# A two-layer hybrid diffusion trunk: adaLN row sums on VectorE with a broadcast silu, and the inverse's small products issued round the array's tiles

## The chip, the cores and the metric

The kernel runs on one core of one Trainium2 chip. The metric is the device time of one execution in microseconds (us), as the median of the runs shown. TensorE is called PE, VectorE DVE, ScalarE ACT, GpSimd POOL; SP only issues the DMAs.

## The reference, cut to what matters

Two layers of a trunk over 512 latent tokens and 256 context tokens, with 1024 channels. Each layer modulates its normed input by vectors that come out of one matrix-vector product (adaLN), mixes by neighbourhood attention, a gated delta rule in chunks and a Fourier mixer, and ends in an MLP.

```python
cs, ccs = jax.nn.silu(c), jax.nn.silu(c_ctx)          # two vectors of 1024
...
sh1, sc1, gt1, sh2, sc2, gt2 = jnp.split((cs @ w_ada + b_ada)[:, None, :], 6, axis=-1)   # w_ada 1024 x 6144 a layer
n_mod = 6 if ctx_out else 2                           # the last layer needs two of the six for the context
cmod = jnp.split((ccs @ w_ada[:, :n_mod * d] + b_ada[:n_mod * d])[None, None, :], n_mod, axis=-1)
h_l = _rmsnorm(x, norm1) * (1 + sc1) + sh1
...
a_mat = strictly lower part of (kb @ k.T * decay) + eye(64)     # one for each chunk of 64 tokens, head and direction
sol = lax.linalg.triangular_solve(a_mat, rhs, left_side=True, lower=True)
...
x = x + gt1 * y_l
x = x + gt2 * _sq_relu_mlp(_rmsnorm(x, norm2) * (1 + sc2) + sh2, w_mlp1, w_mlp2)
```

All arithmetic is f32. The modulation needs 6144 sums of 1024 products a layer, once for the latent tokens and once for the context.

## The kernel before, in words

Activations lie channel-major: a tile has 128 channels on the partitions and 512 (latent) or 768 (latent and context) tokens along the row. Every weight tile is split into two rounded parts, `whi` (cast on ACT, line 233) and `wlo` (subtracted on DVE or POOL, line 236), and a projection is three matmuls for each of 8 contraction tiles (`proj`, line 245). There are 4 buffers of raw weights (`wr`) and 3 of split ones, each half a unit (4 contraction tiles).

The program runs start, layer 0, layer 1. A layer has three stretches: the Fourier mixer and the first head's input; the mix, in which four streams (delta rule, its preparation, attention, input projections) are interleaved by `by_clock`; and the main stretch, with the gated merge of three branches (loop over `bi`), the output projection (`ps_wo`), the second norm (`mod_norm`) and the MLP (`ps_m`). In the merge each of 8 tiles `k` takes a gate (`ps_in`, computed there for the first branch, read back as `sgg` for the others) and a branch product (`ps_br`); lines 1082 to 1085 multiply and add them on DVE, and line 253 splits the sum `y` into `ysh`, `ysl` for the output projection. A list scheduler in the framework sets the order on each engine by the program's order as priority and by its own estimate of readiness; each engine then works through its list in order.

**adaLN.** 4 blocks of 512 outputs are made at the start (`ada_block`). The other 20 blocks are made in layer 0's main stretch: a generator, `ada_rest`, is advanced by `ada_tick` (ADA_RATE 0.6 steps for each projection unit), and by `ada_upto` where a result is due. `ada_group` makes 4 blocks at a time: for each of 8 contraction tiles it loads four tiles of `w_ada` (128x512) and issues four matmuls onto the array's four column strips, which hold the two silu vectors as a 32-column weight (line 168); then ACT copies the sums (172), four small matmuls against `sel8` turn them into columns (176), and DVE adds the bias (178).

**The inverse.** For each head and layer, `dn_prep` inverts 12 unit lower triangular 128x128 tiles (two 64-token chunks each): DVE inverts the 32x32 diagonal blocks of all at once (lines 581, 583), DMAs put them back as diagonal blocks, and PE merges. First 32 to 64: 24 products for R (line 601, a loop over two places q of the array, ACT copy 603 after each), then 36 for W (609, 613, again one place after the other, copies 616 and 617). Then 64 to 128: 12 products (625), and 6 at one place (630) and 6 at another (636), each with its PSUM tile and copy. An f32 product is two records in the trace.

Of the kernel before, what the change touches and what calls it, by code (L numbers as in the profile page):

```python
# [9 lines left out]
F32 = mybir.dt.float32  # L10
# [7 lines left out]
P = 128  # L18
D = 1024
# [12 lines left out]
WRAW, WSPLIT, WADA = 4, 3, 8  # L32
# [4 lines left out]
ADA_RATE, ADA_LAG = 0.6, 1  # L37
# [7 lines left out]
def kernel(ctx: ExitStack, tc: tile.TileContext, A: dict, out: bass.AP):  # L45
# [18 lines left out]
    def U(name, dt=F32, tag="u", w=TT):  # L64
        b, n = cur[tag]
        return b.tile([P, w], dt, tag=tag, bufs=n, name=name)
# [21 lines left out]
    def ps_aux(name, tag="pa"):  # L88
        b, n = cur["ps"]
        return b.tile([P, 512], F32, tag=tag, bufs=n[tag], name=name)  # L90

    def cload(name, shape, src):
        t = const.tile(shape, F32, name=name)
        sp.dma_start(out=t, in_=src)
        return t
# [17 lines left out]
    sel8 = cload("sel8", [P, 8], A["sel8"])  # L113
# [42 lines left out]
    def ada_group(l, q, lag):  # L156

        ps = ps_aux("ps_ada")
        ws = []
        for t in range(KD + lag):  # L160
            if t < KD:
                ws.append([U("wada", tag="wada", w=512) for _ in range(4)])
                for j in range(4):
                    sp.dma_start(out=ws[t][j], in_=A["wa"][l, q + j, t])
            if t >= lag:
                k = t - lag
                for j in range(4):
                    pe.matmul(ps[32 * j:32 * j + 32, :], lhsT=cs[:, k, :], rhs=ws[k][j], start=(k == 0),
                              stop=(k == KD - 1), tile_position=(0, 32 * j))
            yield  # L170
        asb = tp.tile([P, 512], F32, tag="t2", name="asb")
        act.copy(asb, ps)
        yield
        pm = ps_aux("ps_ada2")
        for i in range(4):
            pe.matmul(pm[:, 8 * i:8 * i + 8], lhsT=asb[:, i * P:(i + 1) * P], rhs=sel8, start=True, stop=True)
        b = vecs[l][:, V_BADA + 4 * q:V_BADA + 4 * q + 16].rearrange("p (j i) -> p j i", i=4)
        dve.tensor_tensor(MOD[l][:, 4 * q:4 * q + 16, :].rearrange("p (j i) s -> p j i s", i=4),
                          pm[:, 0:32].rearrange("p (i j s) -> p j i s", i=4, s=2),
                          b.unsqueeze(3).to_broadcast([P, 4, 4, 2]), op=ALU.add)  # L180
# [3 lines left out]
    def ada_scale(l, i, k0=0, n=KD):  # L184

        sc = MOD[l][:, (3 * i + 1) * 8 + k0:(3 * i + 1) * 8 + k0 + n, :]
        g = vecs[l][:, (V_N1, V_N2)[i] + k0:(V_N1, V_N2)[i] + k0 + n]
        o = SC[l][i][:, k0:k0 + n, :]
        dve.tensor_scalar(o, sc, 1.0, None, op0=ALU.add)
        dve.tensor_tensor(o, o, g.unsqueeze(2).to_broadcast([P, n, 2]), op=ALU.mult)  # L190

    def ada_rest():
        for l, qs, sc in ((0, (4, 8), (1,)), (1, (0, 4, 8), (0, 1))):
            for q in qs:
                yield from ada_group(l, q, ADA_LAG)
                ada_done.append((l, q + 3))
            for i in sc:
                ada_scale(l, i)
        ada_done.append((2, 0))
        while True:  # L200
            yield
# [163 lines left out]
    def layer(l):  # L365
# [158 lines left out]
        def dn_prep(h, st):  # L524
# [71 lines left out]
            R = U("R", tag="pr", w=NU * 64).rearrange("p (u c) -> p u c", c=64)  # L596
            ps = ps_aux("ps_r", "pp")
            for q in range(2):
                a, b = slice(64 * q, 64 * q + 32), slice(64 * q + 32, 64 * q + 64)
                for u in range(NU):  # L600
                    pe.matmul(ps[a, u * 32:u * 32 + 32], lhsT=Nu[b, u, a], rhs=Tst[b, u, b], start=True, stop=True,
                              tile_position=(64 * q + 32, 64 * q))
                act.copy(R[a, :, 0:32], ps[a, 0:NU * 32].rearrange("p (u c) -> p u c", c=32))
            ps = ps_aux("ps_w", "pp")
            for q in range(2):
                a, b = slice(64 * q, 64 * q + 32), slice(64 * q + 32, 64 * q + 64)
                ul = slice(0, NU) if q == 0 else slice(6, NU)
                for u in range(ul.start, ul.stop):
                    pe.matmul(ps[b, u * 32:u * 32 + 32], lhsT=R[a, u, 0:32], rhs=Nu[a, u, a], start=True, stop=True,
                              tile_position=(64 * q, 64 * q + 32))  # L610
                ut = slice(0, 6) if q == 0 else slice(0, NU)
                for u in range(ut.start, ut.stop):
                    pe.matmul(ps[a, u * 32:u * 32 + 32], lhsT=Nu[a, u, a], rhs=R[a, u, 0:32], start=True, stop=True,
                              tile_position=(64 * q, 64 * q))
                pv = ps[:, 0:NU * 32].rearrange("p (u c) -> p u c", c=32)
                act.activation(out=Nu[b, ul, a], in_=pv[b, ul], func=AF.Copy, scale=-1.0)
                act.activation(out=Tst[a, ut, b], in_=pv[a, ut], func=AF.Copy, scale=-1.0)
# [11 lines left out]
            for u in range(6):  # L629
                pe.matmul(ps[a, u * 64:u * 64 + 64], lhsT=Nu[a, u, a], rhs=R[a, u, :], start=True, stop=True,  # L630
                          tile_position=(0, 0))
            act.activation(out=Tst[a, 0:6, b], in_=ps[a, 0:384].rearrange("p (u c) -> p u c", c=64), func=AF.Copy,
                           scale=-1.0)
            ps = ps_aux("ps_w3", "pp")
            for u in range(6):
                pe.matmul(ps[b, u * 64:u * 64 + 64], lhsT=R[a, 6 + u, :], rhs=Nu[a, 6 + u, a], start=True, stop=True,
                          tile_position=(0, 64))
# [418 lines left out]
        main_scope = scope("main", u=27, t3b=3, wada=WADA)  # L1056
# [53 lines left out]
        ada_upto(*((0, 11), (2, 0))[l])  # L1110
        mh, ml = mod_norm(l, 1, x2, W, "m")
        fin = None if full else Rms(TL, ps_rms())
# [62 lines left out]
    for half in range(2):  # L1175
        k0, k1 = 4 * half, 4 * half + 4
        for q in (half, half + 2):
            ada_block(0, q)
        ada_scale(0, 0, k0, 4)
        if half == 0:  # L1180
            load_wab(0)
            ahead[0, T_DNK] = wload(A["wi"][0, T_DNK])
        hs += [modulate(k, xs[k]) for k in range(k0, k1)]
        layer.h = tuple(zip(*hs))
        if half == 0:
            for (s0, s1), ps, pb in zip(ALL, begun["in"], begun["ab"]):
                proj(ps, ahead[0, T_DNK], KD, *layer.h, [(s0, s1)], s0, 0, k1)
                proj_ab(pb, *layer.h, s0, s1, 0, k1)
    ident = cload("ident", [P, P], A["ident"])
# [13 lines left out]
def _prepare(inp):  # L1203
# [16 lines left out]
    r["wa"] = a["w_ada"].reshape(2, KD, P, 12, 512).transpose(0, 3, 1, 2, 4)  # L1220
# [53 lines left out]
    r["sel8"] = (i[:, None] // 32 * 2 + i[:, None] % 32 == np.arange(8)[None]) & (i[:, None] % 32 < 2)  # L1274
# [21 lines left out]
```

## Time and profile before

| | us |
|---|---|
| median of 3 runs (lowest, highest) | 2735.25 (2735.04, 2742.7) |
| profiled execution, its own time | 2732.88 |
| span of its instructions | 2731.1 |
| PE / DVE / ACT / POOL busy in it | 2567.2 / 1405.7 / 1191.6 / 619.5 |
| layer 0 mix, 200 to 755: PE / DVE busy | 513.7 / 379.8 of 555 |
| layer 0 main, 755 to 1480: PE / DVE busy | 722.0 / 237.8 of 725 |
| layer 1 mix, 1700 to 2250: PE / DVE busy | 497.6 / 370.4 of 550 |

The profiled execution's own time is 1.8 us above its span, and 2.4 us under the median. [...] A timeline row gives start and duration in us, then the group; a span of pipelined matmuls contains overlaps, so that the start of the next group tells more than a duration. In the groups by shape, the last figure ahead of the bar's end is the mean in ns of one.

### The profile page before, as it was taken

Reading aid. Unit: us, or ns where it says so; the run is one execution under the profiler, and the core shown is the slowest. Engines: PE = TensorE matmul, PEld = TensorE weight load, DVE = VectorE, ACT = ScalarE, POOL = GpSimd, SP = SyncE. Lnnn points to the kernel's source line nnn. Section 1 sums busy time; section 2 is a strip of 40 time slices with the busy share of each in tenths; the row PEclk is TensorE's granted clock in tenths of the full one; section 3 lists DMA queues with packets and bytes.
Section 4 is the critical chain, followed back from the end, with each engine's and each line's share of the span. In section 5 each row is a group of like instructions: output and inputs, shape, how many; then the busy total and the mean of one; then the engine's idle time right before and its main releaser. Section 6 shows DMA issues by size and latency. Waiting matters only on the chain. (4 is left out here: it accounts for less than half of the span.)

```text
span 2731.1 us, 40072 instructions
## 1 busy us (share of the span) xinstructions
PE 2567.2 (94%) x15066; PEld 2083.0 (76%) x15066; DVE 1405.7 (51%) x2847; ACT 1191.6 (44%) x2430; POOL 619.5 (23%) x522
## 2 busy tenths in 40 slices
PE   6998989899999999999999988898999999999998
PEld 3787868687888777888888867776777777688886
DVE  4657586858423634222222355769688436433334
ACT  4546555555644224122222255555565653423323
POOL 3221313131111112111111123322333222222222
PEclk9999999999999999999999999999999999999999
DMA  6232222222256743342321213232232336233322
GB/s 216 78 96 65 70 66 81 72 64 60 74 197 197 254 137 110 105 135 89 120 63 62 82 59 110 78 83 59 79 86 67 94 115 196 87 97 97 97 93 89
DMA packets 196706, 278.42 MB, mean 102 GB/s; under 512 B 56768, under 2 KB 75936, under 8 KB 196512
## 3 DMA queue, kind: packets, MB, share of 16 engines
q1 hardware_dynamic: 196512, 275.87, 32.6%
q8 instruction: 118, 1.93, 0.3%
q14 instruction: 76, 0.62, 0.1%
HBM read 244.29 MB, written 27.31 MB: 99 GB/s over the span
## 5 line engine op out<-in xcount | busy, mean ns | idle before, releaser
L236 POOL TENSOR_TENSOR wlo<-wr,whi 128x512 fp32r<-128x512 f32 x360 | 496.3, 1380 | 1849.8 <-ACT whi L233 1725.3
L233 ACT CAST whi<-wr 128x512 fp32r<-128x512 f32 x560 | 346.3, 619 | 869.5 <-PE ps_m L245 519.8
L245 PE MATMUL ps_in<-hh,whi 128*128 128x512 f32 x960 | 376.8, 403 | 10.5 <-ACT hh L325 4.7
L245 PE MATMUL ps_in<-hh,wlo 128*128 128x512 f32 x960 | 372.6, 399 | 0.8 <-POOL wlo L236 0.8
L245 PE MATMUL ps_in<-hl,whi 128*128 128x512 f32 x960 | 371.1, 397 | 0.0
L236 DVE TENSOR_TENSOR wlo<-wr,whi 128x512 fp32r<-128x512 f32 x200 | 138.6, 693 | 244.6 <-ACT whi L233 243.9
L245 PE MATMUL ps_m<-ml,whi 128*128 128x512 f32 (+1 forms) x768 | 233.9, 358 | 4.7 <-POOL ml L313 3.3
L245 PE MATMUL ps_m<-mh,whi 128*128 128x512 f32 (+1 forms) x768 | 232.6, 357 | 2.9 <-ACT mh L309 2.9
L245 PE MATMUL ps_m<-ah,wlo 128*128 128x512 f32 (+1 forms) x776 | 234.4, 355 | 0.0
L245 PE MATMUL ps_m<-ah,whi 128*128 128x512 f32 (+1 forms) x776 | 234.1, 355 | 0.0
L245 PE MATMUL ps_m<-al,whi 128*128 128x512 f32 (+1 forms) x776 | 233.1, 353 | 0.0
L245 PE MATMUL ps_m<-mh,wlo 128*128 128x512 f32 (+1 forms) x768 | 231.8, 355 | 0.0
L245 PEld LDWEIGHTS ps_in<-hh,whi 128*128 128x128 f32 x960 | 179.3, 191 | 42.9 <-ACT hh L325 4.8
L245 PEld LDWEIGHTS ps_in<-hh,wlo 128*128 128x128 f32 x960 | 178.5, 191 | 33.0 <-issue 1.6
L245 PEld LDWEIGHTS ps_in<-hl,whi 128*128 128x128 f32 x960 | 179.0, 191 | 30.5 <-issue 2.2
L1135 DVE SCALAR_TENSOR_TENSOR x<-ps_m,mod,x 128x512 f32<-128x512 f32 (+1 forms) x97 | 60.8, 654 | 248.1 <-PE ps_m L245 248.1
L245 PEld LDWEIGHTS ps_m<-mh,whi 128*128 128x128 f32 x768 | 126.4, 188 | 35.4 <-ACT whi L233 8.4
L245 PE MATMUL ps_inc<-hl,whi 128*128 128x256 f32 x512 | 149.8, 293 | 0.0
L245 PEld LDWEIGHTS ps_m<-ah,whi 128*128 128x128 f32 x776 | 127.7, 188 | 28.9 <-ACT whi L233 6.7
L245 PEld LDWEIGHTS ps_m<-ml,whi 128*128 128x128 f32 x768 | 126.7, 188 | 29.8 <-POOL ml L313 6.1
L245 PE MATMUL ps_inc<-hh,whi 128*128 128x256 f32 x512 | 149.3, 292 | 0.0
L245 PE MATMUL ps_inc<-hh,wlo 128*128 128x256 f32 x512 | 148.1, 289 | 0.0
(325 smaller groups left out, 4928.9 us busy)
## 6 DMA issues: line engine op xcount, KB each, us to landing
wr<-in_w_dram SPq DMA_DIRECT2D x256, 256.0 KB
wr<-in_wi_dram SPq DMA_DIRECT2D x224, 256.0 KB
wada<-in_wa_dram SPq DMA_DIRECT2D x192, 256.0 KB
wr<-in_wb_dram SPq DMA_DIRECT2D x48, 256.0 KB
wr<-in_wo_dram SPq DMA_DIRECT2D x32, 256.0 KB
gpre<-sgp SPq DMA_DIRECT2D x16, 384.0 KB
sgg<-gpre SPq DMA_DIRECT2D x16, 384.0 KB
rot<-kn SPq DMA_DIRECT2D x64, 64.0 KB
```

The costliest lines, as they stand in the source:

```text
L233: act.copy(hi, raw)
L236: eng.tensor_tensor(lo, raw, hi.bitcast(F32), op=ALU.subtract)
L245: pe.matmul(ps[:, s0 - off:s1 - off], lhsT=a, rhs=b[k][:, s0:s1], start=(k == 0 and i == 0), stop=(k == kn - 1 and i == 2))
L1135: dve.scalar_tensor_tensor(x2[k][:, s0:s1], in0=ps[:, s0:s1], scalar=mod(l, 5, k, v), in1=x2[k][:, s0:s1], op0=ALU.mult, op1=ALU.add)
```

## The change

- The 20 later blocks no longer use PE. `w_ada` is given a second time, transposed (`wat`), so that a tile holds 128 outputs on the partitions and their 1024 weights along the row (512 KB). For each such tile and each conditioning vector DVE does one scalar_tensor_tensor over 128x1024 that multiplies the tile by the silu vector and sums along the row (`accum_out`). The silu, broadcast to all partitions, is `csb` (1 MB): two DMAs at the start write it element by element to `csd` in memory, one DMA reads it back when the main stretch begins.
- Layer 1's context blocks that no one uses are left out: 64 + 32 + 32 = 128 of these DVE instructions, on 80 tiles, with 20 bias adds. A step of the generator is one tile (up to two instructions), and ADA_RATE is 0.85. Buffers: 3 of 4 KB a partition for the tiles, instead of 8 of 2 KB. The main stretch of layer 1 allots none.
- `ada_upto` before the second norm asks for block 9 instead of 11, and for 11 behind it, in layer 0 alone.
- In the inverse the loops over u and over the places are swapped, so that products that follow each other lie in different tiles of the array; the copies come after all of them. The two groups of 6 share one PSUM tile and alternate.

```diff
-WRAW, WSPLIT, WADA = 4, 3, 8
+WRAW, WSPLIT = 4, 3
-ADA_RATE, ADA_LAG = 0.6, 1
+ADA_RATE = 0.85
...
-    def ada_group(l, q, lag):
...
-                for j in range(4):
-                    pe.matmul(ps[32 * j:32 * j + 32, :], lhsT=cs[:, k, :], rhs=ws[k][j], start=(k == 0),
-                              stop=(k == KD - 1), tile_position=(0, 32 * j))
...
+    csd = drp.tile([2, KD, P], F32, name="csd")
+
+    def ada_cond():
+        cb = U("csb", tag="csb", w=2 * D)
+        sp.dma_start(out=cb, in_=csd.rearrange("v k p -> (v k p)").unsqueeze(0).to_broadcast([P, 2 * D]))
+        cur["csb"] = cb
+
+    def ada_block_rows(l, q):
+
+        nv = 2 if l == 0 or q < 4 else 1
+        for i in range(4):
+            w = U("wada", tag="wada", w=D)
+            sp.dma_start(out=w, in_=A["wat"][l, 4 * q + i])
+            for v in range(nv):
+                junk = U("jada", tag="jada", w=D)
+                dve.scalar_tensor_tensor(junk, in0=w, scalar=1.0, in1=cur["csb"][:, v * D:v * D + D], op0=ALU.mult,
+                                         op1=ALU.mult, accum_out=MOD[l][:, 4 * q + i, v:v + 1])
             yield
...
     def ada_rest():
+        ada_cond()
+        for l, q0 in ((0, 4), (1, 0)):
+            for q in range(q0, 12):
+                yield from ada_block_rows(l, q)
+                ada_done.append((l, q))
...
-            for q in range(2):
-                a, b = slice(64 * q, 64 * q + 32), slice(64 * q + 32, 64 * q + 64)
-                for u in range(NU):
+            quads = [(q, slice(64 * q, 64 * q + 32), slice(64 * q + 32, 64 * q + 64)) for q in range(2)]
+            for u in range(NU):
+                for q, a, b in quads:
                     pe.matmul(ps[a, u * 32:u * 32 + 32], lhsT=Nu[b, u, a], rhs=Tst[b, u, b], start=True, stop=True,
                               tile_position=(64 * q + 32, 64 * q))
+            for q, a, b in quads:
                 act.copy(R[a, :, 0:32], ps[a, 0:NU * 32].rearrange("p (u c) -> p u c", c=32))
...
+            uls, uts = (slice(0, NU), slice(6, NU)), (slice(0, 6), slice(0, NU))
+            for u in range(NU):
+                for q, a, b in quads:
+                    if uls[q].start <= u:
+                        pe.matmul(ps[b, u * 32:u * 32 + 32], lhsT=R[a, u, 0:32], rhs=Nu[a, u, a], start=True, stop=True,
+                                  tile_position=(64 * q, 64 * q + 32))
+                for q, a, b in quads:
+                    if u < uts[q].stop:
+                        pe.matmul(ps[a, u * 32:u * 32 + 32], lhsT=Nu[a, u, a], rhs=R[a, u, 0:32], start=True, stop=True,
+                                  tile_position=(64 * q, 64 * q))
...
             for u in range(6):
                 pe.matmul(ps[a, u * 64:u * 64 + 64], lhsT=Nu[a, u, a], rhs=R[a, u, :], start=True, stop=True,
                           tile_position=(0, 0))
+                pe.matmul(ps[b, u * 64:u * 64 + 64], lhsT=R[a, 6 + u, :], rhs=Nu[a, 6 + u, a], start=True, stop=True,
+                          tile_position=(0, 64))
...
-        ada_upto(*((0, 11), (2, 0))[l])
+        if l == 0:
+            ada_upto(0, 9)
         mh, ml = mod_norm(l, 1, x2, W, "m")
+        if l == 0:
+            ada_upto(0, 11)
...
+    for v in range(2):
+        sp.dma_start(out=csd[v].rearrange("k p -> p k"), in_=cs[:, :, v])
```

How the scheduler places it. (Line numbers after the change are up to 3 lower or higher than before.) First DVE in the merge's first branch of layer 0, two tiles k long; L126 (L125 after) is the gate's sigmoid, L1082 (L1080) the product of gate and branch, `jada` the thrown-away product of the row sums. Before:

```order
L1082 TENSOR_TENSOR y<-sgg,ps_br 128x768
L236 TENSOR_TENSOR wlo<-wr,whi 128x512
L126 SCALAR_TENSOR_TENSOR sgg<-ps_in,sgg 128x768
L1082 TENSOR_TENSOR y<-sgg,ps_br 128x768
L236 TENSOR_TENSOR wlo<-wr,whi 128x512 x2
L126 SCALAR_TENSOR_TENSOR sgg<-ps_in,sgg 128x768
```

After:

```order
L1080 TENSOR_TENSOR y<-sgg,ps_br 128x768
L176 TENSOR_TENSOR mod_116<-mod_116,vecs_89 128x8
L171 SCALAR_TENSOR_TENSOR jada,mod_116<-wada,csb 128x1024 x2
L233 TENSOR_TENSOR wlo<-wr,whi 128x512
L171 SCALAR_TENSOR_TENSOR jada,mod_116<-wada,csb 128x1024 x5
L125 SCALAR_TENSOR_TENSOR sgg<-ps_in,sgg 128x768
L171 SCALAR_TENSOR_TENSOR jada,mod_116<-wada,csb 128x1024
L1080 TENSOR_TENSOR y<-sgg,ps_br 128x768
```

Eight row sums stand between one product and the next in this branch; 56 of the 128 stand up to its end, 77 up to the last split of y, 110 up to the second norm's first instruction, and the last 18 in the first units of the MLP.

Then SP in the same place, where `wr` is a weight half and `wada` a tile of `w_ada`. Before:

```order
L164 DMA wada<-in_wa_dram 128x512 x8
L230 DMA wr<-in_wi_dram 128x512 x2
L230 DMA wr<-in_wb_dram 128x512
L164 DMA wada<-in_wa_dram 128x512 x4
L230 DMA wr<-in_wi_dram 128x512 x2
L230 DMA wr<-in_wb_dram 128x512
```

After:

```order
L168 DMA wada<-in_wat_dram 128x1024
L227 DMA wr<-in_wi_dram 128x512
L168 DMA wada<-in_wat_dram 128x1024 x2
L227 DMA wr<-in_wi_dram 128x512
L168 DMA wada<-in_wat_dram 128x1024 x2
L227 DMA wr<-in_wb_dram 128x512
L168 DMA wada<-in_wat_dram 128x1024
```

The tiles of `w_ada` now alternate with the weight halves, one or two at a time.

Last PE in the first head's inverse of layer 0, the W products (L609 and L613). Before:

```order
L609 MATMUL ps_w<-N,R 32x32 x12
L613 MATMUL ps_w<-R,N 32x32 x6
L830 MATMUL ps_sc<-ks,qd 128x256
L831 MATMUL ps_sc<-ks,ql 128x256
L245 MATMUL ps_in<-hl,whi 128x512
L245 MATMUL ps_in<-hh,wlo 128x512
L245 MATMUL ps_in<-hh,whi 128x512
L609 MATMUL ps_w<-N,R 32x32 x6
L613 MATMUL ps_w<-R,N 32x32 x12
```

After:

```order
L599 MATMUL ps_r<-Tst,N 32x32 x23
L829 MATMUL ps_sc<-ks,ql 128x256
L242 MATMUL ps_in<-hh,whi 128x512
L242 MATMUL ps_in<-hl,whi 128x512
L242 MATMUL ps_in<-hh,wlo 128x512
L242 MATMUL ps_in<-hh,whi 128x512
L609 MATMUL ps_w<-N,R 32x32
L613 MATMUL ps_w<-R,N 32x32 x2
L609 MATMUL ps_w<-N,R 32x32
L613 MATMUL ps_w<-R,N 32x32 x2
```

The two bursts of 18 have become one of 36 in which the tile changes with every product; the R products, two bursts of 12 before, are one of 23 behind a first one that stands 16 rows ahead.

## Rows read from the trace of the kernel before

**Rows 1.** Windows of mix 0, main 0, mix 1: PE, PEld, DVE, ACT, POOL; clock; DMA.
```profile
200.00:755.00 555.00, 513.73 (x3650) 424.96 (x3648) 379.77 (x982) 316.83 (x747) 124.00 (x109) 0.98 0.24 69
755.00:1480.00 725.00, 721.95 (x4140) 588.94 (x4141) 237.75 (x306) 206.56 (x310) 110.52 (x83) 1.00 0.42 136
1700.00:2250.00 550.00, 497.64 (x3222) 394.74 (x3223) 370.41 (x946) 311.72 (x720) 160.91 (x132) 0.97 0.29 81
```
**Rows 2.** Windows of line 168, then of line 176, alone: PE and PEld busy.
```profile
750.00:1490.00 740.00, 46.75 (x320) 7.03 (x320) 1.00 0.41 135
750.00:1490.00 740.00, 4.77 (x40) 4.87 (x40) 1.00 0.41 135
```
**Rows 3.** Timeline of PE round one batch of line 168.
```profile
790.25 0.51 PE L245 MATMUL ps_in<-hh,wlo 128*128 128x512 f32 x2
790.69 1.06 PE L168 MATMUL ps_ada<-wada,cs 128*32 128x512 f32 x8
791.69 0.50 PE L245 MATMUL ps_br<-obh,whi 128*128 128x512 f32 x1
```
**Rows 4.** Windows of the merge (three) and the output projection.
```profile
759.00:868.00 109.00, 109.00 (x638) 87.40 (x637) 27.40 (x34) 45.79 (x64) 15.56 (x12) 1.00 0.55 182
868.00:902.00 34.00, 34.00 (x195) 27.14 (x191) 23.26 (x26) 9.51 (x14) 4.09 (x4) 1.00 0.79 267
902.00:940.00 38.00, 38.00 (x228) 29.00 (x226) 23.47 (x26) 9.96 (x14) 3.98 (x4) 1.00 0.80 263
940.00:1020.00 80.00, 80.00 (x462) 64.58 (x454) 26.74 (x39) 20.18 (x30) 12.74 (x10) 1.00 0.46 152
```
**Rows 5.** Groups by shape on DVE: busy us, mean ns, then idle.
```profile
L487 DVE SCALAR_TENSOR_TENSOR kn<-cy,r_l 128x512 f32<-128x512 f32 x16 | 11.1, 691 | 23.1 <-ACT r_l L484 23.0
L468 DVE SCALAR_TENSOR_TENSOR cy<-cin,vecs,cy 128x770 f32<-128x770 f32 x80 | 86.6, 1083 | 1.1
L798 DVE CUSTOM_DVE_ANT_0 Pm<-ps_s,bias,s 128x256 f32<-128x256 f32 x64 | 30.1, 471 | 0.4
L798 DVE DVE_READ_ACCUMULATOR2_ANT s<- 128x1 f32 x64 | 4.8, 76 | 0.0
```
**Rows 6.** Timeline: the last y on DVE, and PE's first output projection.
```profile
944.69 0.51 PE L245 MATMUL ps_wo<-ysh,whi 128*128 128x512 f32 x2
945.04 0.51 PE L245 MATMUL ps_wo<-ysl,whi 128*128 128x512 f32 x2
945.88 1.50 DVE L1085 TENSOR_TENSOR y<-y,sgg 128x768 f32<-128x768 f32 x1
948.28 0.96 DVE L253 TENSOR_TENSOR ysl<-y,ysh 128x768 fp32r<-128x768 f32 x1 [0.90 <-ACT ysh L252]
```
**Rows 7.** Timeline of PE in the first head's inverse.
```profile
253.06 0.94 PE L601 MATMUL ps_r<-Tst,N 32*32 32x32 f32 x24
255.85 0.21 PE L613 MATMUL ps_w<-R,N 32*32 32x32 f32 x1
255.96 0.45 PE L613 MATMUL ps_w<-R,N 32*32 32x32 f32 x9
265.50 0.91 PE L636 MATMUL ps_w<-N,R 64*64 64x64 f32 x12
```
**Rows 8.** Groups by shape on PE: the 32x32 products of the whole run.
```profile
L601 PE MATMUL ps_r<-Tst,N 32*32 32x32 f32 x384 | 15.6, 195 | 0.0
L609 PE MATMUL ps_w<-N,R 32*32 32x32 f32 x288 | 12.0, 192 | 0.0
L613 PE MATMUL ps_w<-R,N 32*32 32x32 f32 x288 | 12.0, 192 | 0.0
```
**Rows 9.** Waits of PE between 200 and 720: us in total, times, longest.
```profile
PE ps_l L482 <- ACT r_l L477: 10.4, 4, 4.0
```
**Rows 10.** The start: a window, and ACT's timeline.
```profile
45.00:50.00 5.00, 4.27 (x32) 1.76 (x34) 0.17 (x1) 0.59 (x1) 0.00 (x0) 1.00 0.01 2
58.02 1.12 ACT L233 CAST whi<-wr 128x512 fp32r<-128x512 f32 x2
```

## What the change should do to the time

> **What bounds the kernel now.** I read the stretches by window first [rows 1], since the whole span's shares are means over unlike stretches, then what the touched lines cost inside them [rows 2, 3], then the engine that receives the work [rows 4 to 6]. The reader should see in [rows 1] that layer 0's main stretch has PE idle for 3.0 of 725 us: there PE sets the end, and whatever leaves PE shortens the stretch unless someone else becomes late. The two mixes have PE idle for 41 and 52 of some 550 us, so PE is short of work there for a tenth of the time, with waits of several us at a time on ACT and DVE, such as 10.4 us in 4 waits for one square [rows 9]. A us of PE saved in a mix is worth less than one in the main stretch. All the adaLN work that the change moves lies in the main stretch of layer 0, where DVE is busy for 238 of 725 us; all the inverse's products lie in the mixes.
>
> **adaLN off PE.** The removed matmuls occupy PE alone for 46.75 us (320 records, 40 batches of eight, 1.17 us each), and the small products behind them for 4.77 us [rows 2]. The timeline shows that this is time and not overlap: between the last projection record ahead and the first behind, one batch takes the array from 790.69 to 791.69 [rows 3]. Forty times 1.00 us and 4.77 is 44.8 us as the lower end; 51.5 us is the upper, and I take it, since each batch also delays its neighbours' starts (about 0.1 us ahead of it). The five copies of the sums on ACT and five bias adds on DVE go too; both engines idle there, so they are worth nothing.
>
> **adaLN on DVE.** 128 sums over 128x1024. The trace has no such instruction. The nearest row is the same operation with two f32 operands from SBUF and no sum, 128x512 in 691 ns; another of 770 elements takes 1083 ns on average; 256 elements with a sum, one operand from PSUM, take 471 ns, and the read of the accumulator 76 ns more [rows 5]. Lower bound: from 256 to 512 elements 220 ns are added, so 1024 would take 691 + 440, with the read 1.21 us. Upper bound: 1083 scaled to 1024 elements is 1.44, with the read 1.52 us. I take 1.3 us, near to the 128x512 row, since it is the same form: twice 691 less one fixed part of about 0.15, plus the read. In all 166 us, which DVE has room for in 725. But the order does not spread them evenly: 77 of the 128 stand ahead of the last split of y, 33 in the output projection, 18 in the MLP. So I make DVE's account up to that split. Before, it was busy 27.4 + 23.3 + 23.5 us in the three windows of the merge [rows 4], some 7 us more for the last two tiles (for each 1.50 and 0.96 [rows 6] and a product of about 0.96), and the change adds 2 us of bias adds: 83 us. With 77 x 1.3 = 100 it is 183 us. PE reaches its first output projection at 944.69 and needs the eighth split 22 pairs of records later, one every 0.35 us [rows 6], at 952.4, which is 193 us after 759. Of these some 20 us go with the adaLN batches (0.6 x 32 units = 19 steps, about 17 batches at 1.17 us), so PE would be there after 174 us. DVE comes 9 us late if it never idles before; PE's three PSUM tiles and three split halves hide a part of that on the way but not at this place, where the eighth split is what PE waits for. I put **8 us of new wait** there. With 1.21 us it is 2 us, with 1.52 us 26 us. The output projection then has 33 sums (43 us) beside about 23 us of old work in 74 us of PE [rows 4], which just fits, so the norm behind it starts on time.
>
> Who stands behind the sums on DVE: `wlo`, the gate's sigmoid and the branch products, for which PE waits at one remove. Up to seven sums in a row (9 us) stand ahead of one of them; three PSUM tiles and three split halves of 4.2 us are the cover. On SP each tile of 512 KB waits for one of three buffers, and the weight halves queue behind it; they are issued some 7 halves (29 us) ahead of PE, which hides it. If that cover is gone it costs a few us in the first branch, inside the upper end above.
>
> **The silu in memory.** 2048 elements of 4 bytes are written at the start, ahead of `ident` to `normf` and the next weights on SP's queue. The DMA engines are idle right after (busy share 0.01 from 45 to 50), and the weights behind are first used by ACT at 58.02, where ACT comes from other work [rows 10]. I take 0, at most +5 us. The read back (1 MB) comes when the merge begins, and only sums wait for it.
>
> **The inverse.** Its 32x32 products are busy for 15.6 + 12.0 + 12.0 us in the run [rows 8] and the two groups of six for 8 x 2 x 0.91 = 14.5 us [rows 7], 54 us in all. In one tile a record starts every 33 ns (24 records in 0.94 us, the last 0.19 long). Where W passes from one tile of the array to the next, records of both tiles start in turn, seven of them between 255.85 and 255.96 [rows 7]: 18 ns each. If all go at that pace, 54 us become 30, a saving of 24. Since the mixes are bound by PE for only a part, and the saved time cannot be used where PE waits for DVE or ACT anyway, I count half of it: **12 us**. On the other side the first copy of R now comes after all 24 products, and the second place needs the last DMAs, so the chain through an inverse may get longer by up to 1 us; 8 times 1 us is the loss if nothing is gained. Bounds: -24 to +8.
>
> [...]
>
> **The sum,** against the profiled execution's own 2732.9 us: -51.5 (PE), +8 (DVE late at the output projection), -12 (inverse), 0 (start) = 2677.4 us. The median shown is 2.4 us above that execution, so I forecast **2680 us**, 2.0% faster.
>
> **Rivals.**
> 1. *Row sums at 1.5 us.* DVE and POOL share work there: the same add of 128x768 took 1.50 us at 945.88 [rows 6], beside a split of the same size in 0.96. For: two operands from SBUF each. Against: POOL is busy for 15% of the stretch only [rows 1]. New wait 26 instead of 8: 2698 us.
> 2. *The products do not run side by side, or the mixes do not care.* PE's waits in the mix are on DVE and ACT [rows 9]. Then the term is 0: 2692 us.
> [...]
> 4. *The start or SP's queue eats the gain piecemeal* (late weights, tiles of `w_ada` behind them): within 0.3% of before only if all of the upper ends come together.
>
> **How the numbers follow.** Forecast 0.50 (2680, own range 2668 to 2690), rival 1 0.15 (2698), rival 2 0.22 (2692), rival 3 0.10 (2783), rival 4 0.03. A measurement of this kernel tells about 0.3% (8 us) from no change. So faster 0.87, same 0.03, slower 0.10. The range goes from 2 us of wait with the whole 24 us of the inverse (2732.9 - 51.5 + 2 - 24 + 2.4 = 2662) to 26 us of wait with nothing from the inverse (2710); rival 3 is left out. Range 2661 to 2710.
>
> **What would show it.** Right: line 171 at 1.2 to 1.4 us in 128 instructions; layer 0's main stretch about 43 us shorter with PE still without idle, except for some us just behind the merge; R, W and the pairs of six in about half of their PE time; the mixes together some 12 us shorter. Wrong: sums of 2 us or more, or PE idle on `wlo`, `ysl` or DVE's products through the whole merge; mixes of the old length although the products got shorter; a wait of PE for `wr` or on DVE for `wada`.

## The result, and the profile after

| | before | after |
|---|---|---|
| median (lowest, highest), us | 2735.95 (2735.04, 2742.7) | 2700.28 (2694.59, 2704.14) |
| ratio, 95% interval | | 0.9863 [0.9849, 0.9877] |
| profiled execution, its own time / span | 2732.88 / 2731.1 | 2694.59 / 2692.8 |

The changed kernel is 1.4% faster; 2.0% was forecast. The profiled execution is the fastest of its four. PE is busy for 71 us less than before:

```profile
PE 2495.8 (93%) x14706; PEld 2055.1 (76%) x14706; DVE 1575.6 (59%) x3118; ACT 1186.7 (44%) x2425; POOL 628.4 (23%) x522
```

but the span fell by 38.3 only. I cut layer 0's main stretch at four events that both kernels have: the first `ps_br` record, the first `ps_wo` record, the first `ps_m` record (start of the MLP), and the first write of `xmid` near the MLP's end. Windows of the kernel before (columns as in [rows 1]: start and end, length, then PE, PEld, DVE, ACT, POOL busy with the number of instructions, the granted TensorE clock as a share of full speed, the DMA engines' mean busy share, GB/s):

```profile
763.90:944.70 180.80, 180.80 (x1051) 143.07 (x1050) 75.47 (x84) 64.68 (x91) 24.80 (x19) 1.00 0.65 213
944.70:1023.90 79.20, 79.20 (x446) 61.90 (x444) 26.97 (x42) 21.69 (x34) 11.58 (x9) 1.00 0.48 158
1023.90:1534.60 510.70, 508.00 (x2915) 424.60 (x2915) 151.35 (x199) 132.54 (x204) 80.62 (x60) 1.00 0.30 96
```

The same three stretches of the changed kernel:

```profile
754.20:928.30 174.10, 162.57 (x914) 141.06 (x913) 168.92 (x243) 62.08 (x87) 29.20 (x19) 0.97 0.74 239
928.30:1012.10 83.80, 73.60 (x394) 60.71 (x392) 75.09 (x117) 20.70 (x34) 13.66 (x9) 0.92 0.77 250
1012.10:1497.90 485.80, 482.05 (x2742) 420.29 (x2743) 177.78 (x235) 131.18 (x201) 83.94 (x60) 1.00 0.25 78
```

The MLP gained 24.9 us; its share of [rows 2] (lines 168 and 176 in that window of before) was 21.07 + 2.86 = 23.9. Merge and output projection together went from 260.0 to 257.9 us, though the other 25.68 + 1.91 = 27.6 us left PE there. PE, which had no idle time in these two stretches, now stands idle for 11.5 and 10.2 us, and its clock is no longer full; DVE is busy for 168.9 of 174.1 us and 75.1 of 83.8. DVE has become the bound of this stretch, and it is full from the merge's first branch on (90.1 of 93.4 us):

```profile
754.20:847.60 93.40, 92.40 (x528) 80.54 (x527) 90.07 (x133) 40.75 (x56) 18.12 (x11) 1.00 0.71 231
```

What PE waited for in the two stretches (us in total, times, longest):

```profile
PE ps_br L242 <- ACT obh L249: 10.6, 2, 10.5
PE ps_rms L273 <- ACT sq L271: 4.2, 1, 4.2
PE ps_rms L272 <- DVE acc L266: 3.8, 1, 3.8
```

One wait of 10.5 us stands between the merge's first and second branch, and 8 us at the norm behind the output projection, where the squares wait for the last `x` from DVE. ACT's row there shows it (in brackets the idle time ahead of the row and what ended it):

```profile
1005.06 0.94 ACT L271 ACTIVATE sq<-x 128x512 f32<-128x512 f32 x2 [7.47 <-DVE x L1103]
```

The first wait names ACT; ACT's own timeline tells why it was late:

```profile
842.43 0.85 ACT L126 ACTIVATE sgg<-sgg 128x768 f32<-128x768 f32 x1 [6.55 <-DVE sgg L125]
...
857.00 0.84 ACT L126 ACTIVATE sgg<-sgg 128x768 f32<-128x768 f32 x1 [8.55 <-DVE sgg L125]
857.75 1.55 ACT L249 CAST obh<-ob 128x768 fp32r<-128x768 f32 x2
```

The gate's exponential (line 126) waits for DVE's step of the sigmoid (line 125), longer with every tile, 8.55 us at the last. In the kernel before (line 127 there) it waited for 1.03 us at most, and for 1.02 at the last tile:

```profile
865.42 0.85 ACT L127 ACTIVATE sgg<-sgg 128x768 f32<-128x768 f32 x1 [1.02 <-DVE sgg L126]
```

Behind the last exponential in ACT's queue stand the casts of the next branch's input (line 249), and for these PE waits:

```profile
847.63 0.51 PE L242 MATMUL ps_br<-obh,wlo 128*128 128x512 f32 x2
858.62 2.29 PE L242 MATMUL ps_br<-obh,whi 128*128 128x512 f32 x6 [10.47 <-ACT obh L249]
```

The sums themselves (DVE busy, min/median/max in ns; the second row is the read of the sum):

```profile
L171 DVE SCALAR_TENSOR_TENSOR jada<-wada,csb x128: 1209/1224/2722, 759.1 to 1067.6; 128x1024 f32<-128x1024 f32 x128
L171 DVE DVE_READ_ACCUMULATOR jada<-wada,csb x128: 74/81/85, 760.3 to 1068.7; 128x1 f32 x128
```

The inverse's products, over the whole run by tile, each instant of PE counted once (`ps_r` with 192 records of line 625 that were not changed; `ps_w` with the groups of six). First `ps_r`, then `ps_w`, before:

```profile
0.00:2731.00 2731.00, 30.32 (x576) 26.19 (x576) 15.04 (x32) 0.98 0.33 102
0.00:2731.00 2731.00, 34.05 (x768) 30.08 (x768) 20.64 (x48) 0.98 0.33 102
```

After:

```profile
0.00:2692.00 2692.00, 24.36 (x576) 20.16 (x576) 15.04 (x32) 0.98 0.34 104
0.00:2692.00 2692.00, 15.33 (x768) 13.29 (x768) 20.64 (x48) 0.98 0.34 104
```

That is 24.7 us less PE time for the same records (6.0 for `ps_r`, 18.7 for W and the sixes).

### The profile page after: what moved, and what is told of

Same layout as the page of the kernel before. It is cut to its first block, busy times and chain, and to the rows that moved or that the text cites. A ratio compares the mean times of both kernels' runs of the same rounds, so it can differ in the third digit from the quotient of the medians.

```text
span 2692.8 us, 39472 instructions
## 1 busy us (share of the span) xinstructions
PE 2495.8 (93%) x14706; PEld 2055.1 (76%) x14706; DVE 1575.6 (59%) x3118; ACT 1186.7 (44%) x2425; POOL 628.4 (23%) x522
## 5 line engine op out<-in xcount | busy, mean ns | idle before, releaser
L233 POOL TENSOR_TENSOR wlo<-wr,whi 128x512 fp32r<-128x512 f32 x360 | 503.9, 1402 | 1775.6 <-ACT whi L230 1588.3
L242 PE MATMUL ps_in<-hh,whi 128*128 128x512 f32 x960 | 376.6, 403 | 12.2 <-DMA wada<-in_wa_dram 4.7
L242 PE MATMUL ps_m<-ah,wlo 128*128 128x512 f32 (+1 forms) x776 | 234.3, 355 | 0.0
L171 DVE SCALAR_TENSOR_TENSOR jada<-wada,csb 128x1024 f32<-128x1024 f32 x128 | 168.1, 1313 | 9.0 <-DMA wada<-in_wat_dram 7.2
L242 PE MATMUL ps_inc<-hl,whi 128*128 128x256 f32 x512 | 148.3, 290 | 0.0
```

The costliest lines, as they stand in the source:

```text
L171: dve.scalar_tensor_tensor(junk, in0=w, scalar=1.0, in1=cur["csb"][:, v * D:v * D + D], op0=ALU.mult, op1=ALU.mult, accum_out=MOD[l][:, 4 ...
L233: eng.tensor_tensor(lo, raw, hi.bitcast(F32), op=ALU.subtract)
L242: pe.matmul(ps[:, s0 - off:s1 - off], lhsT=a, rhs=b[k][:, s0:s1], start=(k == 0 and i == 0), stop=(k == kn - 1 and i == 2))
```

## The experiments

Times are medians; each ratio is against runs of the kernel before on the same chip.

### Each part alone

Before with the new adaLN and the old inverse (`e1_rows_only`), and with the new inverse and the old adaLN (`e2_inverse_only`); the edits are the two halves of the diff above.

> The kernel before with the row sums of adaLN on VectorE alone; the inverse's products stay in their old order. Theory A (read from the two traces: layer 0 from the merge to the end of its MLP gained 27 us instead of 43.5, and the start lost 3): the sums bring about 24 us, so 2712 us (2706 to 2718), and the wait of PE at the end of the merge's first branch, 10.5 us in the changed kernel, is there too. Theory B (the terms of the prediction: -51.5 + 8): 2692 us, with that wait made by the inverse's new order further up. Under both, PE's busy time of the adaLN lines behind the start is 0 instead of 51.5 us.

> The kernel before with the inverse's products in the new order alone; adaLN stays on TensorE. Theory A: the products' own PE time falls from 54 to about 25 us, and the two mixes are shorter by 16 us together (13 and 3 in the traces): 2720 us (2716 to 2724). Theory B (the prediction's term, half of what PE saves at 18 ns a start): 2724. Rival: the mixes are bound by DVE and ACT and what they gained came by the sums' part of the change: 2733 to 2736.

The sums alone: 2708.45 us, 0.9896 [0.9882, 0.9910], some 28 us. The inverse alone: 2721.37 us, 0.9944 [0.9932, 0.9956], 12 to 19 us, centre 15. Together they would be 44; the changed kernel gains 34 to 41, which their intervals allow. The sums came out where theory A had them (2706 to 2718), and theory B's 2692 us is out; for the inverse the rival (2733 to 2736) is out, while theory A's 2720 and theory B's 2724 can't be told apart. Theory A's stall is in the first kernel, 11.0 us on `obh`, so the inverse has no part in it:

```profile
PE ps_br L242 <- ACT obh L249: 11.0, 2, 10.6
```

with the main stretch the same as in the changed kernel (174.4, 84.1 and 485.7 us instead of 174.1, 83.8 and 485.8).

The inverse's gain shows in one mix alone. In the trace of the new inverse by itself layer 0's mix, from the first `Df` to the first `ps_br`, falls from 618.7 to 606.5 us. Behind `xmid`, where layer 1's mix lies, that kernel needs 1196.9 us and the kernel before 1196.5; the expectation had 3 us of gain there, and the kernels with the new inverse scatter by 6.

### Is it DVE's time, or the loads?

The tiles for the sums are 42 MB on SP's queue and the DMA engines. The kernel before loaded as much for its blocks, but more of it later: the DMA share rose from 0.65 and 0.48 in merge and output projection to 0.74 and 0.77. Two kernels part DVE's time from the loads. `e6_short_sums` keeps the loads and sums 128 of each tile's 1024 columns; `e8_few_loads` keeps the sums at full length and loads a quarter of the tiles.

```diff
-                dve.scalar_tensor_tensor(junk, in0=w, scalar=1.0, in1=cur["csb"][:, v * D:v * D + D], ...
+                dve.scalar_tensor_tensor(junk[:, 0:P], in0=w[:, 0:P], scalar=1.0, in1=cur["csb"][:, v * D:v * D + P], ...
```

```diff
-            w = U("wada", tag="wada", w=D)
-            sp.dma_start(out=w, in_=A["wat"][l, 4 * q + i])
+            if i == 0:
+                w = U("wada", tag="wada", w=D)
+                sp.dma_start(out=w, in_=A["wat"][l, 4 * q])
```

> The changed kernel with every sum over 128 of its 1024 columns (the rest of each adaLN sum is left out); the loads of w_ada stay whole. Theory A (VectorE's time is what the merge pays for): a sum takes 0.3 instead of 1.39 us, VectorE gets 120 us back up to the norm, the stall at the branch's end and those at the norm go, and merge with output projection fall from 258 to 234 to 240 us: 2676 to 2684 us. Rival B (the loads, with a DMA share of 0.72 to 0.77, and the SP queue are what it pays for): stays at 2696 to 2705.

> The changed kernel with one load of w_ada for four rows of tiles instead of four (three quarters of the weights are left out; the sums take the same tile again): 20 loads of 512 KB instead of 80, all 128 sums of full length. Theory A (VectorE's time): merge and output projection stay at 254 to 260 us, VectorE as full as in the changed kernel, sums at 1.3 us: 2696 to 2702 us. Rival B (loads and SP queue): 15 to 20 us faster, 2680 to 2686. If the long sums of 2.2 us come from the loads' writes to memory, their share falls; if from GpSimd's operations, it stays.

Short sums: 2680.82 us, 0.9797 [0.9775, 0.9819]. A sum takes 0.29 us there, and 0.08 us for its read (in the changed kernel the 110 sums up to the norm took 144.4 us with their reads, 1.31 each and not the 1.39 of the expectation), and merge and output projection fall to 169.6 and 74.1 us, with the DMA engines busier than ever (0.88 in the first window):

```profile
755.40:925.00 169.60, 162.50 (x915) 141.62 (x914) 109.84 (x312) 61.54 (x87) 25.74 (x19) 0.97 0.88 304
925.00:999.10 74.10, 70.90 (x393) 59.80 (x392) 37.38 (x91) 21.29 (x34) 11.83 (x9) 1.00 0.75 255
```

Few loads: 2695.5 us, 0.9848 [0.9829, 0.9867]. That is half a us under theory A's 2696 to 2702 and far from rival B's 2680 to 2686. At a DMA share of 0.49 and 0.43 the stretch is as long as ever and DVE as full:

```profile
755.30:928.70 173.40, 161.68 (x915) 140.50 (x913) 168.39 (x243) 61.98 (x87) 30.39 (x19) 0.97 0.49 155
928.70:1013.60 84.90, 73.84 (x394) 60.68 (x392) 81.94 (x128) 20.46 (x34) 13.72 (x9) 0.92 0.43 137
```

So DVE's time is the cause in the changed kernel; the loads are not. What theory A had wrong is that short sums still leave 7.1 us of wait on `obh` (the stretch came out at 243.7 us, where 234 to 240 were expected). The framework then puts 82 sums ahead of the eighth `y` instead of 56, and DVE waits for their loads 47 times, 57.3 us together; that this is where the 7.1 us come from is likely, but no run shows it.

### One buffer

The cheapest way to hold sums back: `"wada": 1` in place of `"wada": 3`.

> The changed kernel with one buffer for the tiles of w_ada instead of three; by the order of its instructions 28 sums instead of 56 then stand ahead of the eighth y on VectorE, and 72 instead of 110 ahead of the norm, the rest in the MLP. Theory A: the 10.5 us of PE idle at the end of the first branch come from VectorE being full there (91 of 92 us busy); with 28 sums less (39 us) it has room, the stall falls under 2 us, the waits at the norm under 4, and the whole is 12 to 18 us faster than the changed kernel: 2682 to 2688 us. Rival: one buffer makes each load wait on the SP queue for the sum before, with the weights queued behind it; PE then waits for weights through the merge and it is 5 to 20 us slower: 2705 to 2720. Second rival: the stall is ACT's own (its order) and stays: 2698 to 2702.

2714.07 us, 0.9921 [0.9903, 0.9939], slower than the changed kernel: the rival won on the size, but not by its mechanism. 28 sums less stood in the first branch, and the stall on `obh` halved to 5.3 us; but DVE, which works in order, now waits for tiles itself, 27 times, and PE waits for the `wlo` that stand behind such sums (in the first of PE's rows 8.0 us at once, at the output projection). Waits of DVE, then of PE, up to the MLP:

```profile
DVE jada L171 <- DMA wada<-in_wat_dram: 53.0, 27, 5.0
```

```profile
PE ps_wo L242 <- DVE wlo L233: 8.0, 1, 8.0
PE ps_br L242 <- DVE wlo L233: 8.0, 3, 3.2
PE ps_br L242 <- ACT obh L249: 5.3, 1, 5.3
```

The SP queue, which the rival named, would show as waits of PE for ACT's `whi`; up to the MLP there is none. The MLP, into which 56 sums went, also got 15 us longer (501.1). Sums must come later *and* with their tiles in place.

### The border's casts moved ahead in ACT's queue

`e7_splits_early` writes the next branch's loads and splits ahead of the sixth gate:

```diff
             for k in range(KD):
+                if k == 5 and bi < 2:
+                    nxt = load_ob(obs[bi + 1][0])
                 sg = T3("sgg")
```

> The changed kernel with the next branch's four splits written two and a half tiles earlier (ahead of the sixth gate of a branch instead of behind its eighth), so that ACT casts them before the last gates' exponentials. Theory A (VectorE's lag reaches PE through ACT's queue): the 10.5 us wait of PE on obh is gone, but VectorE is as full as before and some of it comes back at the splits of y or the norm; 3 to 8 us faster than the changed kernel: 2692 to 2697. Rival 1 (the lag is only moved): 2699 to 2702, with a new wait of about 10 us on VectorE behind the merge. Rival 2 (the queue is all there is to it): 2689 to 2691.

2695.45 us, 0.9842 [0.9821, 0.9864]; the intervals of this and of the changed kernel overlap. The mechanism shows in the trace: the wait on `obh` is gone, the merge fell from 174.1 to 166.0 us, and the output projection with the norm grew from 83.8 to 89.9. What PE waits for now:

```profile
PE ps_rms L273 <- ACT sq L271: 5.0, 1, 5.0
PE ps_rms L272 <- DVE acc L266: 3.1, 1, 3.1
PE ps_wo L242 <- ACT ysh L249: 2.8, 1, 2.8
```

ACT's queue is the way by which DVE's lag reaches PE at the border, not the cause; with it opened, 8.1 us are saved and 6.1 paid behind. The 2.0 us left are less than theory A's 3 to 8: most of the lag is only moved, as rival 1 said, though not to one wait of 10 us.

### Sums held back by data

In `e5_paced` each step makes a 1.0 out of what DVE finished last, and its sums take that as their scalar, so that the framework can't put them ahead; a sum takes 1.28 us with it, 1.22 without. The rate is even over merge and output projection; block 11 is asked for only behind the first eight units of the MLP.

```diff
-ADA_RATE = 0.85
+ADA_RATE = 0.62, 0.9
...
+            tok = U("tok", tag="tokb", w=1)
+            dve.tensor_scalar(tok, after[:, 0:1], 0.0, 1.0, op0=ALU.mult, op1=ALU.add)
+            cur["tok"] = tok
...
-                dve.scalar_tensor_tensor(junk, in0=w, scalar=1.0, ...
+                dve.scalar_tensor_tensor(junk, in0=w, scalar=cur["tok"], ...
```

> The changed kernel with its sums tied to the program's progress: each step writes a 1.0 out of the tile that VectorE finished last (128x1), and the sums of that step take it as their scalar, so that they can't be placed ahead of it. Three buffers as before. By the order 18 sums instead of 56 stand ahead of the eighth y, 39 instead of 77 ahead of the last split of y, 54 instead of 110 ahead of the norm, and 74 in the MLP. Theory A: merge and output projection (258 us from the first ps_br to the first ps_m, as long as before the change) are set by VectorE, 244 of 258 us busy; with 56 sums less (75 us) PE sets the end again, the stretch falls to 236 to 242, the MLP grows by at most 4, and the whole is 12 to 20 us faster than the changed kernel: 2680 to 2688 us. Rival: loads for sums that wait hold the SP queue and the weights behind it, as with one buffer: 2705 to 2720.

2696.71 us, 0.9860 [0.9836, 0.9883]: no gain, neither by theory A nor with the rival's loss. The MLP took its 74 sums for nothing (484.8 us), the border was mended (2.9 us on `obh`), but a new wait stands ahead of the output projection, and DVE is full in branches two and three (71.5 of 80.9 us):

```profile
846.00:926.90 80.90, 71.86 (x385) 60.86 (x386) 71.54 (x106) 20.16 (x31) 12.82 (x8) 0.96 0.64 202
926.90:937.50 10.60, 1.58 (x11) 1.12 (x9) 10.60 (x16) 2.17 (x3) 1.43 (x1) 0.78 0.45 151
```

```profile
PE ps_wo L246 <- DVE wlo L237: 9.0, 1, 9.0
```

An even rate is wrong, since DVE's room is uneven: a tile of the first branch takes PE 11.5 us (it computes its gate) and DVE some 3.4 without sums; one of the later branches takes PE 5.1 us and DVE some 3.5 (23.3 us in 34, [rows 4]).

### Sums placed by DVE's room

`e9_paced_early` changes the rates of `e5_paced` and places the sums so: 34 in the first branch, none in the second, three towards the end of the third, 15 up to the norm, 76 in the MLP; with the early splits and the silu in pieces of 32 bytes (below). `e10_paced_late` is the same with the splits in their old place.

```diff
-ADA_RATE = 0.62, 0.9
+ADA_RATE = 1.1, 0, 0.8, 0.9
```

> The changed kernel with three things: the sums tied to the program's progress as in the paced kernel, but placed by VectorE's room (1.1 tiles of w_ada a step in the first branch, none in the second and third, 0.8 a step in the output projection, 0.9 a step in the MLP, so 34 sums ahead of the eighth y, 37 ahead of the last split of y, 52 ahead of the norm); each branch's splits written two and a half tiles early; the silu written in pieces of 32 bytes. Theory A (VectorE's account by branch: a tile of the first branch takes PE 11.5 us and VectorE 3.4 without sums; a tile of the second and third takes PE 5.1 and VectorE 3.5, so room for hardly one sum): no wait of PE above 3 us up to the norm, the stretch from the first ps_br to the first ps_m falls from 258 to 238 to 244 us and the MLP stays at 485: 2675 to 2683 us. Rival (the loads that wait for a sum hold the weights on the SP queue, or VectorE's order in the output projection is what costs): stretch at 250 or more, 2690 or more.

> As the kernel with sums placed by VectorE's room, but each branch's splits in their old place, behind the eighth gate. Theory A (VectorE isn't late any more at the end of the first branch, so the place of the splits matters little): 2677 to 2686, with at most 3 us of wait on obh. Rival (the border stands by ACT's queue alone, whatever VectorE does; the kernel with short sums had 7.1 us there): a wait of 6 to 8 us on obh and 2684 to 2690.

2672.62 us, 0.9759 [0.9738, 0.9780], and 2674.21 us, 0.9772 [0.9758, 0.9787]: both beat the kernel before and the changed one, by 2.3 to 2.4% and about 1%, and both came a little under what theory A had (2675 to 2683 and 2677 to 2686). The three stretches of the first:

```profile
762.50:923.30 160.80, 160.02 (x914) 139.52 (x913) 126.70 (x187) 63.27 (x89) 27.85 (x19) 1.00 0.61 195
923.30:996.80 73.50, 70.48 (x394) 59.83 (x392) 48.48 (x84) 20.73 (x33) 12.40 (x9) 1.00 0.51 169
996.80:1481.70 484.90, 481.76 (x2742) 420.89 (x2743) 254.47 (x410) 131.61 (x201) 88.15 (x60) 1.00 0.37 117
```

The reader should see PE almost without idle (0.8 us) and at full clock in the merge, DVE at 79% there, and an MLP that is as short with 76 sums as with 18. From the first `ps_br` to the MLP it is 234.3 us instead of 257.9: 23.6 of the 25.5 us that were missing (27.6 left PE there, and 2.1 had come through). With the splits in their old place the wait on `obh` is 1.7 us and the stretch 238.3 us, 4.0 more; the medians can't be told apart. With DVE in time, their place matters little, as theory A said.

### The silu's way to memory

`e4_csd_rows` copies the silu to a compact tile and writes it in 256 pieces of 32 bytes instead of 2048 of 4.

```diff
-    for v in range(2):
-        sp.dma_start(out=csd[v].rearrange("k p -> p k"), in_=cs[:, :, v])
+    csc = const.tile([P, 2, KD], F32, name="csc")
+    pool.tensor_copy(csc, cs[:, :, 0:2].rearrange("p k v -> p v k"))
+    sp.dma_start(out=csd.rearrange("v p k -> p v k"), in_=csc)
```

> The changed kernel, but the silu goes to memory in 256 pieces of 32 bytes (copied to a compact tile first; the columns of w_ada are laid out to match) instead of 2048 pieces of 4 bytes. Theory A: the small pieces hold the SP queue, so that the weights behind them are issued at 48.9 instead of 39.2 us and the first head's work starts 3 us later; with pieces of 32 bytes the issue is back at 39 to 41 us, and the whole 2 to 4 us faster than the changed kernel: 2697 us. Rival: the 3 us come from the clock (0.87 instead of 0.91 between 40 and 80 us) or from where the loads stand, and stay: 2700.

2693.69 us, 0.9841 [0.9827, 0.9856]; its interval and the changed kernel's overlap, and it is faster than either expectation (2697 and 2700). The weights behind are issued at 38.55 instead of 48.94 us, as expected, but that isn't what moves the start. In all twelve traces the load of the first head's `Df` starts the earlier, the higher the clock that PE was granted from 60 to 80 us, wherever the weights were issued. At a clock of 0.83 it starts between 147.8 and 148.3 us (the kernel with the new inverse alone, whose weights are issued at 38.72, is among them); at 0.91, between 145.2 and 147.1 (with the kernel with one buffer, 48.78); at 1.00, between 142.0 and 142.7 (with the kernel with short sums, 47.52, and this one). The clock of two of them, the new inverse alone and this kernel:

```profile
60.00:80.00 20.00, 19.08 (x98) 16.28 (x96) 8.87 (x19) 9.00 (x30) 5.69 (x13) 0.83 0.13 43
```

```profile
60.00:80.00 20.00, 18.31 (x104) 15.26 (x105) 11.32 (x22) 10.61 (x32) 6.40 (x16) 1.00 0.22 68
```

Theory A for the start is thereby refuted. That the clock is the cause fits all twelve traces, but no run changed it by itself, and what decides it in that window was not found out.

## Why the prediction was right, and where not

The time fell inside the range, though not inside the forecast's own 2668 to 2690, and the direction was right. Work left PE in both parts, as argued; the wait that the sums on DVE bring was forecast at a third of its size. The sum came out 17 us low against the profiled execution (2677.4 forecast, 2694.59 measured), and 20 by the medians (2680 and 2700.28). Between the two traces the 38.3 us are 27.0 in the main stretch of layer 0, 12.8 in the mix ahead of it and 1.6 behind `xmid`, less 3.1 at the start. Term by term:

- **adaLN off PE, -51.5: right in size.** The MLP alone got 24.9 us of it, and with sums placed where DVE has room the other half appears too: from the first `ps_br` to the first `xmid` the best kernel needs 719.2 us, the kernel before 770.7, a difference of 51.5. That this agrees to the tenth is chance: PE is busy for 55.7 us less there (712.3 instead of 768.0), more than the upper end of the prediction, and idle for 4.2 more; with the splits in their old place the stretch needs 723.1.
- **DVE late at the output projection, +8: the step that failed.** It was 24.5 us (51.5 less the 27.0 that the same stretch gained, 770.7 to 743.7), and most of it stood at other places. The cost of a sum was right: line 171 occupies DVE for 169.1 us in 128 sums with their reads, 1.32 us each, where 1.3 was forecast. Its fixed part of about 0.15 us shows as well: 0.292 us for 128 columns (`e6_short_sums`) and 1.224 for 1024, medians both, leave 0.16. What was wrong is the account: I balanced DVE from the merge's begin to its end, 183 us against 174, and trusted that three PSUM tiles and three split halves cover everything on the way. By the order of the program 56 of the 77 sums stand in the first branch, where PE takes some 92 us and DVE has 27.4 us of old work [rows 4]; 56 x 1.32 + 27 is 101. DVE was behind by the end of that branch (busy for 90.1 of 93.4 us, with 7.9 us of sums done only while PE stood), and the way to PE was one that I hadn't followed: through ACT, whose exponential of the last gate waits for DVE, to the casts of the next branch queued behind it. I had named the sigmoid among those that stand behind sums, but asked only when PE would need the gate, not what else stands on ACT behind it. "The norm behind it starts on time" failed too: 4.2 and 3.8 us, since 33 sums of 1.32 us and 23 us of old work make 67 us, all of the projection's 67 (928.3 to 995.4, the last `ps_wo`), with nothing left for a DVE that comes in late.
- **The inverse, -12, bounds -24 to +8: right, a little low.** The products go side by side: PE's time for them fell by 24.7 us, where the prediction had 24, and 15 (12 to 19) came through to the end. The half was a guess, and it didn't hold in each mix: in the trace of the new inverse alone layer 0's mix gained 12.2 us, and nothing shows behind `xmid`. That the rest is lost to waits for DVE and ACT, as argued, fits PE's longest waits in layer 0's mix of that kernel (12.2 us for `Pm` from DVE, 8.7 for `r_l` from ACT), but how much they took back was not measured.
- **The start, 0: right for the queue.** The queue is held up by 10 us, and nobody waits: ACT's first cast of the weights behind starts at 57.83 us, and started at 58.02 before [rows 10]. The 3.1 us that the changed kernel lost at the start (`Df` at 148.3 instead of 145.2) go with the clock, 0.83 instead of 0.91 from 60 to 80 us; the kernel with the new inverse alone, which writes no silu, has both.

```profile
57.83 1.13 ACT L230 CAST whi<-wr 128x512 fp32r<-128x512 f32 x2
```

- **Rival 1** (sums at 1.5 us, 2698 us) came nearest to the time by luck: the sums were short, and PE lost nearly its 26 us in another way. **Rival 2** is out: the products run side by side (24.7 us less PE time) and the kernel with the new inverse alone gains 12 to 19 us. **Rival 3** (2783 us) is out: it took a sum at 2.3 us, and no run shows such a cost for the sums in general; they took 1.22 us in the median for 1024 elements, where 512 without a sum took 0.69 [rows 5], and 2.25 us in eleven of 128.
- **The pace of 18 ns a start** was read from W's products; R's have it too. They alternate between two places of the array, in different rows of it, and write one PSUM tile, and 46 of their records took 0.94 us, the time that 24 took at one place [rows 7]; with the last 0.19 long that is a start every 17 ns:

```profile
254.76 0.94 PE L599 MATMUL ps_r<-Tst,N 32*32 32x32 f32 x46
```

## What to carry to other kernels

When work moves to an engine with room, make the account for each stretch between two points at which someone waits for that engine, not for the whole loop: the account over the whole merge had DVE at 183 us in 174, over its first branch alone it is 101 in 92. This framework's scheduler puts instructions without a deadline as early as their buffers allow (56 of the 128 sums stood in the first branch), and they fill the engine in the wrong place. A late engine can reach others through an in-order queue that waits for it once: ACT's exponential waited 8.55 us for DVE, and PE 10.5 us for the casts behind it. Look at what stands behind such a wait. And hold free work back by data it must wait for, with its loads in place, where the receiving engine is slack (2672.62 us); one buffer held it back by making the engine itself wait (DVE 27 times, 53.0 us; 2714.07 us).

## What the runs showed of the hardware

- Some sums on DVE (two operands from SBUF) and subtractions on POOL (two as well) took longer where they met. Eleven of the 128 sums took 2.25 us on average, where the median is 1.22, and all eleven began while POOL was in a subtraction. At 794.34 POOL was in its subtraction, and the sum took 2.20 us; at 798.23 the sum had begun, and POOL's subtraction took 2.01, where the median of line 233 there is 1.29. DVE, then POOL:

```profile
794.34 2.20 DVE L171 SCALAR_TENSOR_TENSOR jada<-wada,csb 128x1024 f32<-128x1024 f32 x1
...
797.85 1.23 DVE L171 SCALAR_TENSOR_TENSOR jada<-wada,csb 128x1024 f32<-128x1024 f32 x1
```

```profile
794.04 1.41 POOL L233 TENSOR_TENSOR wlo<-wr,whi 128x512 fp32r<-128x512 f32 x1 [11.08 <-ACT whi L230]
798.23 2.01 POOL L233 TENSOR_TENSOR wlo<-wr,whi 128x512 fp32r<-128x512 f32 x1 [2.78 <-ACT whi L230]
```

With a quarter of the loads the share of long sums was not smaller (15 of 128), so the loads are not what makes them.

- Small products in different tiles of the array, issued in turn, took between two fifths and two thirds of the PE time that they took one tile after the other: at the first inverse the 72 records of W occupy PE for 0.95 us instead of 2.44; over the run R's 384 records take 9.5 us instead of 15.6.
- The stall of PE between the first two branches cost its length and a piece of clock behind it. After the 10.5 us without work PE's first records ran at a granted clock of 0.50, and from 862.7 on at 1.00:

```profile
858.60:862.20 3.60, 3.58 (x11) 3.11 (x12) 3.56 (x7) 0.70 (x1) 0.00 (x0) 0.50 0.86 313
862.70:880.00 17.30, 17.25 (x97) 14.65 (x97) 15.66 (x23) 5.63 (x8) 1.42 (x2) 1.00 0.81 263
```

In the two stretches in which PE idled the mean granted clock was 0.97 and 0.92, and PE was busy for 5.7 us longer than in `e9_paced_early`, the best kernel, with the same work (162.6 and 73.6 against 160.0 and 70.5 us).

- The clock granted from 60 to 80 us differed between 0.83 and 1.00 among kernels with nearly the same work there (PE busy for 18.3 to 19.1 us), and the load of the first head's `Df` started between 148.3 and 142.0 us with it. Outside the parts that were changed the kernels differ as much in other places: the first mix took 606 to 616 us from the first `Df` to the first `ps_br` in the kernels with the new inverse, and the program behind `xmid` 1192 to 1198. The MLP repeats better: all the kernels with sums on DVE need 484.5 to 485.8 us for it, but the one with one buffer.
